# The first FFN product of a hybrid encoder block in Strassen's form, with the norm's factor applied at the end

## The chip, the core and the metric

The kernel runs on one core of one Trainium2 chip. The metric is device time in microseconds (us), as the median of several executions. TensorE (PE; PEld is its weight load) multiplies; VectorE (DVE), ScalarE (ACT) and GpSimd (POOL) do the elementwise work; SyncE (SP) issues the loads from HBM. Each engine takes its instructions in program order, and waits on semaphores for the others.

## The reference, cut to what matters

The input has 512 tokens of 1,024 features. 16 meta tokens are put ahead of them, so L is 528. The last third of the block is what changes:

```python
h = h + jnp.concatenate([y_ret, y_ssd], axis=-1) @ w_out[i]
u = _rmsnorm(h, norm2_w[i]) @ w_ff1[i]          # 1024 -> 4096
h = h + jnp.square(jax.nn.relu(u)) @ w_ff2[i]   # 4096 -> 1024
return _rmsnorm(h, final_norm_w)[:, CHUNK:]
```

Here `_rmsnorm(x, w)` is `x * rsqrt(mean(x*x) + 1e-6) * w` by token.

## The kernel before, in words

**Precision.** Every large product runs on operands split in two: hi is the value rounded to fp32r (an ACT copy, line 151), lo is what is left (a DVE subtraction, line 152). A block of 128 contraction rows then takes three matmuls: hi x hi, lo x hi and hi x lo. A weight load is 1 MB (`wr`, pool `wraw`, two buffers); each half of it is split into one tile `wh` of pool `whl` (three buffers).

**Stages, by the span's clock.** Up to about 420 us come the input projections, the SSD scan and the retention. The output projection `wo` follows in two halves of 512 columns (hf 0 to 470.6, hf 1 to 515.75), then the first FFN product to 697.58, then the second in two halves (`w2`) to about 877, and the last norm's tail.

**`token_gemm`** (wo and w2) holds four PSUM accumulators, one for each 128 tokens. For each of the 128-row blocks k it takes a split of the activations (`mh`, from `split_act`) as the stationary operand, and 512 columns of weights as the moving one. Its last `stag` blocks run as a tail, token block by token block, so that `fin` of one block runs beside the matmuls of the next. `weave` runs such a generator and, at each of its yields, one step of every job in `jobs`; `drain` runs the jobs to their end. So the program order on every engine is that of the emission.

**The first FFN product before.** `fin1` of a token block adds the accumulator to `xt` (line 802) and appends the job `norm_gen`, which applies the whole norm, waits `LAG` yields, transposes and splits into `hnh`/`hnl` (features on partitions). `first_tiles` computes three feature tiles of 128 by 256 tokens at a time (144 matmuls of 256 columns), because the last tokens come late; the other 29 tiles take 24 matmuls of 512 columns each (lines 334 to 336). `relu2` is an ACT relu out of PSUM and a DVE square into `a[f]`. `part`/`ahead` split one tile ahead of its use.

**Layout.** Pools with `side="right"` grow down from address 229,344, the others grow up from behind a scratch area of 16,384 bytes and 128 bytes of constants. From the tile sizes follow the start addresses in each partition: `whl` at 57,600, 66,304 and 75,008, and `mh2` (wo's hf 1) at 120,576 plus multiples of 4,096: all are multiples of 64. `mh` (wo's hf 0) at 154,144, `hnh` at 195,552, `hnl` at 212,448, `mhf` (w2) at 170,976, and of the retention `qr` at 174,752 and `kr` at 180,896 lie 32 bytes past a multiple of 64.

## Time and profile before

| | |
|---|---|
| median of 3 executions | 886.72 us (886.70 to 886.85) |
| profiled execution | 886.82 us, of which 885.0 us are the span from the first instruction to the last |
| mean granted TensorE clock | 0.997 of full speed |

The profile is of one execution. "Idle before" is the time for which an engine stood still ahead of an instruction, with what released it. A matmul's duration is longer than the distance to the next one's start, because matmuls overlap; so what a matmul costs is read from starts. PEclk 1.00 is 2.4 GHz, 0.50 is 1.2 GHz.

### The profile page before, as it was taken

The numbers are of one execution on the slowest core, as the hardware profiler recorded it, in microseconds if no ns is written. First come the engines' busy times: TensorE is split into PE (matmuls) and PEld (weight loads), VectorE is DVE, ScalarE is ACT, GpSimd is POOL, SyncE is SP. The second block draws the span as 40 slices with busy tenths as digits, with TensorE's granted clock in tenths as the row PEclk, the third lists the DMA queues.
The fourth block names the chain that finished last, engine by engine and source line by source line (L and its number), as shares of the span: only waits on it lengthen the run. The fifth ranks groups of instructions, "written<-read, shape, count | busy, mean of one in ns | idle before, by whom it ended". The sixth has DMA issues, their size and how long they took to land.

```text
span 885.0 us, 12244 instructions
## 1 busy us (share of the span) xinstructions
PE 873.3 (99%) x5062; PEld 757.9 (86%) x5062; DVE 488.9 (55%) x813; ACT 354.4 (40%) x602; POOL 34.0 (4%) x66
## 2 busy tenths in 40 slices
PE   8999999999999999999999999999999999999996
PEld 6999999989988999889888898888888888888884
DVE  5789887878654555445465563333333444464442
ACT  5673727372433232323454443222222333353332
POOL 2000000000000000000000010000000000000001
PEclk9999999999999999999999999999999999999998
DMA  8433241333231313222123431222222222222212
GB/s 324 147 122 96 96 127 65 100 93 108 60 96 48 96 51 93 62 81 96 49 96 96 143 119 33 93 90 90 93 89 94 96 94 90 95 94 95 95 49 95
DMA packets 84360, 85.14 MB, mean 96 GB/s; under 512 B 2352, under 2 KB 67120, under 8 KB 84304
## 3 DMA queue, kind: packets, MB, share of 16 engines
...
## 4 chain that ended last, share of the span: by engine, by line
PE 91%; DVE 3%; DMA 2%; ACT 2%; POOL 1%; issue 1%; POOLq 0%; SPq 0%; ACTq 0%; DVEq 0%
PE acc L765 9%; PE acc L763 9%; PE acc L764 9%; PE pf L335 7%; PE pf L336 7%; PE pf L334 7%; PE pz L457 3%; PE pj L334 3%; PE pj L336 3%; PE pj L335 3%; PE pv L334 2%; PE pk L336 2%; PE pv L336 2%; PE pk L334 2%; PE pk L335 2%; PE pv L335 2%
## 5 line engine op out<-in xcount | busy, mean ns | idle before, releaser
L152 DVE TENSOR_TENSOR wh<-wr,wh 128x1024 fp32r<-128x1024 f32 x134 | 163.5, 1221 | 137.4 <-ACT wh L151 137.4
L151 ACT ACTIVATE wh<-wr 128x1024 fp32r<-128x1024 f32 x134 | 141.0, 1055 | 204.0 <-PE acc L765 84.7
L763 PE MATMUL acc<-wh,mh 128*128 128x512 f32 x370 | 146.5, 396 | 0.0
L765 PE MATMUL acc<-wh,mh 128*128 128x512 f32 x370 | 146.0, 395 | 0.0
L764 PE MATMUL acc<-wh,mh 128*128 128x512 f32 x370 | 146.0, 395 | 0.0
L335 PE MATMUL pf<-hnl,wh 128*128 128x512 f32 (+1 forms) x280 | 105.4, 376 | 0.4 <-DVE hnl L152 0.4
L336 PE MATMUL pf<-hnh,wh 128*128 128x512 f32 (+1 forms) x280 | 105.6, 377 | 0.0
L334 PE MATMUL pf<-hnh,wh 128*128 128x512 f32 (+1 forms) x280 | 105.3, 376 | 0.0
L765 PEld LDWEIGHTS acc<-wh,mh 128*128 128x128 f32 x370 | 69.5, 188 | 16.5
L764 PEld LDWEIGHTS acc<-wh,mh 128*128 128x128 f32 x370 | 69.5, 188 | 16.2
L763 PEld LDWEIGHTS acc<-wh,mh 128*128 128x128 f32 x370 | 69.5, 188 | 16.1
L890 DVE TENSOR_TENSOR a<-r 128x512 f32<-128x512 f32 x32 | 22.2, 693 | 106.4 <-ACT r L889 106.4
L334 PE MATMUL pj<-hnh,wh 128*128 128x256 f32 (+2 forms) x256 | 73.6, 288 | 0.0
L336 PE MATMUL pj<-hnh,wh 128*128 128x256 f32 (+2 forms) x256 | 72.8, 286 | 0.0
L335 PE MATMUL pj<-hnl,wh 128*128 128x256 f32 (+2 forms) x256 | 72.8, 284 | 0.0
L889 ACT ACTIVATE r<-pf 128x512 f32<-128x512 f32 x32 | 19.1, 598 | 124.9 <-PE pf L336 124.9
L335 PEld LDWEIGHTS pf<-hnl,wh 128*128 128x128 f32 x280 | 53.0, 189 | 11.4 <-DVE hnl L152 0.7
L334 PEld LDWEIGHTS pf<-hnh,wh 128*128 128x128 f32 x280 | 52.7, 188 | 10.5
L336 PEld LDWEIGHTS pf<-hnh,wh 128*128 128x128 f32 x280 | 52.7, 188 | 10.1
L151 ACT ACTIVATE mh<-a 128x512 fp32r<-128x512 f32 x64 | 39.6, 623 | 34.3 <-PE acc L765 32.9
L152 DVE TENSOR_TENSOR mh<-a,mh 128x512 fp32r<-128x512 f32 x64 | 43.8, 689 | 14.7 <-ACT mh L151 14.7
L335 PEld LDWEIGHTS pj<-hnl,wh 128*128 128x128 f32 x256 | 48.2, 188 | 0.0
...
## 6 DMA issues: line engine op xcount, KB each, us to landing
wr<-in_w_ff_dram SPq DMA_DIRECT2D x32, 1024.0 KB, 5.1
...
wr<-in_w_out_dram SPq DMA_DIRECT2D x8, 1024.0 KB, 4.9
wr<-in_w_in_dram SPq DMA_DIRECT2D x7, 1024.0 KB, 4.9
...
```

Of the source, the lines that this page charges most:

```text
L151: ACT.activation(dst_h, src, AF.Copy)
L152: DVE.tensor_tensor(dst_l, src, dst_h.bitcast(F32), op=ALU.subtract)
L334: PE.matmul(ps[:, :n], lhsT=wh[:, k, :], rhs=hnh[:, k, t0:t0 + n], start=(k == 0), stop=False)
L335: PE.matmul(ps[:, :n], lhsT=wh[:, k, :], rhs=hnl[:, k, t0:t0 + n], start=False, stop=False)
L336: PE.matmul(ps[:, :n], lhsT=wl[:, k, :], rhs=hnh[:, k, t0:t0 + n], start=False, stop=(k == KT - 1))
L457: PE.matmul(o, lhsT=a[:, k, tk], rhs=zp[k // 4][y][:, k % 4, :], start=(i == 0), stop=(i == len(seq) - 1))
L763: PE.matmul(acc[b], lhsT=s[:, 0, tk], rhs=wh[:, kk, :], start=(k == 0), stop=False)
L764: PE.matmul(acc[b], lhsT=s[:, 1, tk], rhs=wh[:, kk, :], start=False, stop=False)
L765: PE.matmul(acc[b], lhsT=s[:, 0, tk], rhs=wl[:, kk, :], start=False, stop=(k == nk - 1))
L889: ACT.activation(r, ps, AF.Relu)
L890: DVE.tensor_tensor(a[f], r, r, op=ALU.mult)
```

## The change

The 4,096 features are taken in 8 groups of 512. In a group, weights and transposed tokens are seen as 2 x 2 blocks: contraction halves, feature halves (256) and token halves (256). Seven products of such blocks replace eight (Winograd's variant of Strassen's form). A product is 24 matmuls of 256 columns: two feature tiles by four contraction blocks by three split terms.

- **Tokens.** `tok_gen` replaces `norm_gen`: it transposes `xt` itself, and ACT copies it out of PSUM with norm2's weight as the scale (four copies of 128x128 for each transposed bank). Four DVE subtractions make the token sums, seven splits (`split_hs`) the operands `HS`.
- **Weights.** Each group has two 1 MB units. Four DVE sums (`s_sum`, 128x1024) per group are made partly in place in the raw tile, and each of the seven blocks is split (`w1_prep`), `LOOK` = 3 products ahead. A raw tile is free when product 3 (its first unit) or products 4 and 7 (its second) are split; only then are `next_loads` issued.
- **Sums of products.** Products 1 and 2 share a bank, 6, 7 and 4 another, 5 and 3 a third. Product 1 is copied out by ACT before product 2 accumulates in the same bank; products 6, 7 (two adds), 4 and 3 are added up by DVE. relu and square are both on ACT, one `product` later (`flush`), in place.
- **Norm.** The factor 1/(mean square + 1e-6) is made by `mean_sq` among the products and applied in `add_h2`, as the scale of the second FFN product's accumulator.
- **Order.** `seq` lists the products; the last two (4 and 3 of group 7) stand between the first steps of the second FFN product.
- **Memory.** `wraw` has 4 buffers, `whl` 4, `nwb` leaves `perm`, `pc` grows by 8 columns, `small` by four tiles, and the scratch area is 1,024 bytes.

```diff
-LAG = 4
+LAG = 2
+LOOK = 3
...
-PC_N = 104
+PC_CW, PC_CB, PC_SN, PC_RN, PC_N1, PC_N2 = 0, 64, 80, 88, 96, 104
+PC_N = 112
...
-    wraw = ctx.enter_context(tc.tile_pool(name="wraw", bufs=2))
-    whl = ctx.enter_context(tc.tile_pool(name="whl", bufs=3))
+    wraw = ctx.enter_context(tc.tile_pool(name="wraw", bufs=4))
+    whl = ctx.enter_context(tc.tile_pool(name="whl", bufs=4))
...
-    nwb = perm.tile([P, D], F32, name="nwb")
...
-    mh2 = tc.alloc_tile_pool(name="mh2", bufs=7, reuse_waits="tile")
+    mh2 = tc.alloc_tile_pool(name="mh2", bufs=6, reuse_waits="tile")
...
+    hnp.release()
...
+    NG = FF // 512
+    ar = tc.alloc_tile_pool(name="ar", bufs=1, side="right", reuse_waits="tile")
+    hs12 = tc.alloc_tile_pool(name="hs12", bufs=1, side="right", reuse_waits="tile")
     wx = tc.alloc_tile_pool(name="wx", bufs=3, side="right", reuse_waits="tile")
-    U[("w1", 0)].pools = [wx, wx]
...
+    HS = {q: hs12.tile([P, 2, 4, 256], F32R, name=f"hs{q}") for q in (1, 2)}
+    a_hi = ar.tile([P, 8, T], F32, name="a_hi")
+    R = [[a_hi[:, 2 * (2 * j + h):2 * (2 * j + h) + 2, :].rearrange("p a b -> p (a b)") for h in range(2)] for j in range(2)]
+    rs2 = [small.tile([P, 1], F32, name=f"rs2{b}", bufs=1) for b in range(NB)]
+    FP = {}
+    def split_hs(q, pool, src):
+        t = HS.get(q)
+        if t is None:
+            t = HS[q] = pool.tile([P, 2, 4, 256], F32R, name=f"hs{q}")
+        split(t[:, 0].rearrange("p k n -> p (k n)"), t[:, 1].rearrange("p k n -> p (k n)"), src)
+    def tok_gen(b):
         for _ in range(LAG):
             yield
-        transpose_split(xns[b], P, b * P)
+        h = b // 2
+        for j in range(2):
+            ps = psum(pm, "tp")
+            for k in range(4):
+                PE.transpose(ps[:, k * P:(k + 1) * P], xt[b][:, (4 * j + k) * P:(4 * j + k + 1) * P], ident)
+            dst = R[j][h].rearrange("p (k n) -> p k n", n=256)[:, :, (b % 2) * P:(b % 2 + 1) * P]
+            for k in range(4):
+                ACT.activation(dst[:, k, :], ps[:, k * P:(k + 1) * P], AF.Copy, scale=pc[:, PC_N2 + 4 * j + k:PC_N2 + 4 * j + k + 1])
+            if b == 1:
+                split_hs(1 + j, None, R[j][0])
+            yield
+        if b < 3:
+            return
+        sub = lambda o, x, y: DVE.tensor_tensor(o, x, y, op=ALU.subtract)
+        t2 = FP["a"][:, 14:16, :].rearrange("p a b -> p (a b)")
+        sub(R[0][0], R[0][1], R[0][0])
+        sub(t2, R[1][1], R[0][0])
+        while "t" not in FP:
+            yield
+        split_hs(6, FP["t"], t2)
+        yield
+        split_hs(5, FP["t"], R[0][0])
+        sub(R[0][1], R[1][1], R[0][1])
+        yield
+        split_hs(7, FP["t"], R[0][1])
+        yield
+        sub(R[1][0], R[1][0], t2)
+        split_hs(4, FP["t"], R[1][0])
+        yield
+        split_hs(3, FP["t"], R[1][1])
...
         add_h(1)(b, acc)
-        jobs.append(norm_gen(b))
-    ws = []
+        jobs.append(tok_gen(b))
...
+    seq = [(1, 0), (1, 1), (2, 0), (2, 1), (1, 2), (2, 2), (6, 0), (5, 0), (7, 0), (6, 1), (4, 0), (5, 1), (3, 0), (7, 1),
+           (6, 2), (4, 1), (5, 2), (3, 1), (7, 2)]
+    for g in range(3, NG):
+        seq += [(1, g), (4, g - 1), (6, g), (3, g - 1), (5, g), (2, g), (7, g)]
+    seq += [(4, NG - 1), (3, NG - 1)]
+    at = {q: i for i, q in enumerate(seq)}
+    raws, wsp, s1s = {}, {}, {}
+    loads = [0, 2, 4, 1, 6, 7] + list(range(8, 2 * NG))
...
+    def w1_load(u, raw=None):
+        if raw is None:
...
+        nc.sync.dma_start(out=raw.rearrange("p (k c) -> p k c", c=256),
+                          in_=w1[:, 256 * u:256 * (u + 1)].rearrange("(k p) c -> p k c", p=P))
+        raws[u] = raw
+    def next_loads():
+        while st1["load"] < len(loads) and (st1["load"] < 4 or loads[st1["load"] - 4] in done):
+            w1_load(loads[st1["load"]])
...
+    def quarter(g, r, c):
+        return raws[2 * g + r][:, c * 1024:(c + 1) * 1024]
+    def s_sum(i, g):
+        if i == 1:
+            s1s[g] = FP["s"].tile([P, 1024], F32, tag="s", name="s1")
+            DVE.tensor_tensor(s1s[g], quarter(g, 1, 0), quarter(g, 1, 1), op=ALU.add)
+        elif i == 3:
+            DVE.tensor_tensor(quarter(g, 1, 0), quarter(g, 0, 0), quarter(g, 1, 0), op=ALU.subtract)
+        elif i == 2:
+            DVE.tensor_tensor(quarter(g, 0, 0), s1s[g], quarter(g, 0, 0), op=ALU.subtract)
+        else:
+            DVE.tensor_tensor(quarter(g, 0, 1), quarter(g, 0, 1), quarter(g, 0, 0), op=ALU.subtract)
...
+    sums = {}
+    for g in range(NG):
+        p = at[(6, g)]
+        for i, q in ((1, p - 6), (3, p - 5), (2, p - 4), (4, max(p + 1, at[(2, g)] - LOOK + 1, at[(3, g)] - LOOK))):
+            sums.setdefault(max(q, 0), []).append((i, g))
+    def w1_prep(n, pool=None):
+        if n >= len(seq) or n in wsp:
+            return
+        q, g = seq[n]
+        src = {1: lambda: quarter(g, 0, 0), 2: lambda: quarter(g, 0, 1), 3: lambda: quarter(g, 0, 1), 4: lambda: quarter(g, 1, 1),
+               5: lambda: s1s[g], 6: lambda: quarter(g, 0, 0), 7: lambda: quarter(g, 1, 0)}[q]()
+        t = (pool or whl).tile([P, 2, 1024], F32R, tag="w", name="wh")
+        split(t[:, 0, :], t[:, 1, :], src)
+        wsp[n] = t.rearrange("p y (k c) -> p y k c", c=256)
+        if q == 3:
+            done.add(2 * g)
+        if all(at[(i, g)] in wsp for i in (4, 7)):
+            done.add(2 * g + 1)
+        next_loads()
...
     def before_tail():
...
+        next_loads()
+        for n in range(LOOK):
+            w1_prep(n, wx)
...
+    def a_block(g, r, h):
+        t, o = (FP["a"], 4 * g) if g < 6 else (a_hi, 4 * (g - 6))
+        return t[:, o + 2 * r:o + 2 * r + 2, h * 256:(h + 1) * 256]
...
+    def relu2(v, src=None):
+        ACT.activation(v, v if src is None else src, AF.Relu)
+        ACT.activation(v, v, AF.Square)
+    def flush():
+        while later:
+            relu2(later.pop(0))
+    def product(n):
+        for e in sums.get(n, ()):
+            s_sum(*e)
+        w1_prep(n + LOOK)
+        flush()
+        q, g = seq[n]
+        bk = {1: "a", 2: "a", 6: "b", 7: "b", 4: "b", 5: "d", 3: "d"}[q]
+        if q in (1, 6, 5):
+            banks[(bk, g)] = psum(pm if bk == "d" else pp, "f" + bk)
+        ps = banks[(bk, g)]
+        w, h = wsp[n], HS[q]
+        for t in range(2):
+            o = ps[:, t * 256:(t + 1) * 256]
+            cs = slice(t * P, (t + 1) * P)
+            for k in range(4):
+                for i, (y, z) in enumerate(((0, 0), (0, 1), (1, 0))):
+                    PE.matmul(o, lhsT=w[:, y, k, cs], rhs=h[:, z, k, :], start=(q in (1, 6, 5) and t == 0 and k == 0 and i == 0),
+                              stop=(k == 3 and i == 2), skip_group_check=True)
+            yield
+        pv = ps.rearrange("p (t n) -> p t n", n=256)
+        if q == 1:
+            ACT.activation(a_block(g, 1, 0), pv, AF.Copy)
+        elif q == 2:
+            relu2(a_block(g, 0, 0), pv)
+        elif q == 6:
+            DVE.tensor_tensor(a_block(g, 0, 1), pv, a_block(g, 1, 0), op=ALU.add)
+        elif q == 7:
+            v = a_block(g, 1, 1)
+            DVE.tensor_tensor(v, pv, a_block(g, 1, 0), op=ALU.add)
+            DVE.tensor_tensor(v, banks[("d", g)].rearrange("p (t n) -> p t n", n=256), v, op=ALU.add)
+            later.append(v)
+        elif q != 5:
+            v = a_block(g, 1, 0) if q == 4 else a_block(g, 0, 1)
+            DVE.tensor_tensor(v, pv, v, op=ALU.add)
+            later.append(v)
...
+    mh2.release()
...
     ap = tc.alloc_tile_pool(name="ap", bufs=1, reuse_waits="tile")
...
+    FP["a"] = ap.tile([P, 24, T], F32, name="a_lo")
+    FP["s"] = tc.alloc_tile_pool(name="fs", bufs=2, reuse_waits="tile")
+    for u, o in ((3, 16), (5, 20)):
+        w1_load(u, FP["a"][:, o:o + 4, :].rearrange("p a b -> p (a b)"))
...
+    def mean_sq(b):
+        jk = FP["s"].tile([P, D], F32, tag="s", name="jk")
+        ACT.activation(jk, xt[b], AF.Square, accum_out=rs2[b])
+        POOL.tensor_scalar(rs2[b], rs2[b], 1.0 / D, EPS, op0=ALU.mult, op1=ALU.add)
+        DVE.reciprocal(rs2[b], rs2[b])
+    def first_products():
+        for n in range(len(seq) - 2):
+            if n == LOOK:
+                wx.release()
+                FP["t"] = tc.alloc_tile_pool(name="hst", bufs=1, side="right", reuse_waits="tile")
+            if n == at[(6, 0)]:
+                drain()
+            if n in range(24, 24 + 4 * NB, 4):
+                mean_sq((n - 24) // 4)
+            yield from product(n)
...
+    def add_h2(hf):
+        def f(b, acc):
+            v = xt[b][:, hf * 512:(hf + 1) * 512]
+            DVE.scalar_tensor_tensor(v, acc, rs2[b], v, op0=ALU.mult, op1=ALU.add)
+        return f
...
+    FP["s"].release()
+    mhs = [tc.alloc_tile_pool(name="mhw", bufs=3, reuse_waits="tile")]
+    pre = [split_act(a_tile(k), mhs[0]) for k in range(3)]
+    second = token_gemm("w2", 0, 32, a_tile, fin_a, 2, mhs, pre, banks=(pp, pp, pp, pm))
+    for n in (0, 1):
+        weave(itertools.islice(second, 2 - n))
+        weave(product(len(seq) - 2 + n))
+    flush()
+    FP["t"].release()
+    hs12.release()
+    fin = tc.alloc_tile_pool(name="fin", bufs=1, side="right", reuse_waits="tile")
+    nwb = fin.tile([P, D], F32, name="nwb")
+    nc.sync.dma_start(out=nwb, in_=nfw.partition_broadcast(P))
+    mhs.append(tc.alloc_tile_pool(name="mhf", bufs=6, side="right", reuse_waits="tile"))
+    ys = tc.alloc_tile_pool(name="ys", bufs=1, reuse_waits="tile")
+    yo += [ys.tile([P, D], F32, name=f"yo{b}") for b in range(NB)]
+    ep += [ys.tile([P, 1], F32, name=f"ep{b}") for b in range(NB)]
+    weave(second)
+    weave(token_gemm("w2", 1, 32, a_tile, fin_b, 4, mhs))
     ys.release()
-    mh.release()
-    hnp.release()
-    fw.release()
+    mhs[1].release()
+    mhs[0].release()
+    fin.release()
+    ar.release()
     ap.release()
@@ -936,6 +1085,7 @@
     pcols[:, PC_SN:PC_SN + 8] = np.asarray(ssd_norm_w)[0].reshape(8, P).T
     pcols[:, PC_RN:PC_RN + 8] = np.asarray(ret_norm_w)[0].reshape(8, P).T
     pcols[:, PC_N1:PC_N1 + 8] = np.asarray(norm1_w)[0].reshape(8, P).T
+    pcols[:, PC_N2:PC_N2 + 8] = np.asarray(norm2_w)[0].reshape(8, P).T
     xall = np.concatenate([np.asarray(meta_tokens), np.asarray(x)[0]]).T.reshape(KT, P, L).transpose(1, 0, 2)
     xtr = np.concatenate([xall[:, :, :272].reshape(P, -1), xall[:, :, 272:].reshape(P, -1)], axis=1)
@@ -943,12 +1093,12 @@
     wzd = np.concatenate([wf[:, C_Z:C_Z + 256], wf[:, C_DT:C_DT + SH]], axis=1).reshape(2, 4, P, 256 + SH).transpose(2, 0, 1, 3)
     rope, mask, cpack, gpow = _constants()
     arrs = {
-        "x": f(x)[0], "meta_tokens": f(meta_tokens), "xtr": xtr, "wzd": wzd, "norm2_w": f(norm2_w)[0],
+        "x": f(x)[0], "meta_tokens": f(meta_tokens), "xtr": xtr, "wzd": wzd,
         "final_norm_w": f(final_norm_w), "w_in": f(w_in)[0], "w_out": f(w_out)[0], "w_ff1": f(w_ff1)[0],
         "w_ff2": f(w_ff2)[0],
         "hrows": np.concatenate([f(d_skip)[0], f(dt_bias)[0], f(a_log)[0]]), "pcols": pcols, "crope": rope, "cmask": mask, "cpack": cpack, "cident": np.eye(P, dtype=np.float32),
     }
-    nc = bacc.Bacc("TRN2", target_bir_lowering=False, num_devices=1)
```

## Rows read from the trace of the kernel before

**Rows 1.** The page: busy time, share of the span and instructions; chain by engine.

```profile
PE 873.3 (99%) x5062; PEld 757.9 (86%) x5062; DVE 488.9 (55%) x813; ACT 354.4 (40%) x602; POOL 34.0 (4%) x66
...
PE 91%; DVE 3%; DMA 2%; ACT 2%; POOL 1%; issue 1%; POOLq 0%; SPq 0%; ACTq 0%; DVEq 0%
```

**Rows 2.** TensorE's waits: waiting line, releaser, us in total, times, longest.

```profile
PE pf L335 <- DVE hnl L152: 0.4, 1, 0.4
```

**Rows 3.** Windows, first FFN product: stretch, length, busy time by engine, clock, DMA share, GB/s.

```profile
600.00:660.00 60.00, 60.00 (x258) 48.46 (x258) 19.87 (x21) 16.87 (x22) 0.00 (x0) 1.00 0.28 88
```

**Rows 4.** Matmuls of 512 columns by line and stretch: ns min/median/max, first and last start.

```profile
L763 PE MATMUL acc<-wh,mh x20: 395/396/397, 455.0 to 468.3; 128*128 128x512 f32 x20
...
L763 PE MATMUL acc<-wh,mh x22: 389/390/390, 471.1 to 485.4; 128*128 128x512 f32 x22
...
L763 PE MATMUL acc<-wh,mh x22: 392/396/397, 720.0 to 734.7; 128*128 128x512 f32 x22
...
L334 PE MATMUL pf<-hnh,wh x22: 392/394/399, 559.7 to 574.4; 128*128 128x512 f32 x22
```

**Rows 5.** Matmuls of 256 columns, first three tiles, the same columns.

```profile
L334 PE MATMUL pf<-hnh,wh x19: 278/280/282, 527.4 to 533.8; 128*128 128x256 f32 x19
```

**Rows 6.** Timeline of TensorE, 30 to 40 us: start, us, line, operation; 24 starts per shape.

```profile
30.48 0.28 PE L334 MATMUL pj<-hnh,wh 128*128 128x260 f32 x1
...
33.34 0.28 PE L334 MATMUL pj<-hnh,wh 128*128 128x256 f32 x1
...
36.18 0.29 PE L334 MATMUL pj<-hnh,wh 128*128 128x272 f32 x1
...
39.19 0.28 PE L334 MATMUL pj<-hnh,wh 128*128 128x256 f32 x1
```

**Rows 7.** Timeline of TensorE, z projection: 21 starts apart.

```profile
175.96 0.28 PE L457 MATMUL pz<-wh,hnl 128*128 128x256 f32 x1
...
178.45 0.28 PE L457 MATMUL pz<-wh,hnl 128*128 128x256 f32 x1
```

**Rows 8.** Matmuls of 128 columns of one retention head.

```profile
L705 PE MATMUL sc<-qr,kr x8: 274/275/276, 430.9 to 431.7; 128*128 128x128 f32 x8
```

**Rows 9.** VectorE by line and form: busy us, mean ns, idle before.

```profile
L152 DVE TENSOR_TENSOR wh<-wr,wh 128x1024 fp32r<-128x1024 f32 x134 | 163.5, 1221 | 137.4 <-ACT wh L151 137.4
L152 DVE TENSOR_TENSOR mh<-a,mh 128x512 fp32r<-128x512 f32 x64 | 43.8, 689 | 14.7 <-ACT mh L151 14.7
...
L802 DVE TENSOR_TENSOR xt<-xt,acc 128x512 f32<-128x512 f32 x16 | 10.7, 682 | 7.2 <-PE acc L765 7.2
```

**Rows 10.** Timeline of VectorE: two splits back to back, 1024 and 512 elements.

```profile
515.71 1.28 DVE L152 TENSOR_TENSOR hnl<-tp,hnh 128x512 fp32r<-128x512 f32 x2
...
517.50 2.35 DVE L152 TENSOR_TENSOR wh<-wr,wh 128x1024 fp32r<-128x1024 f32 x2
```

**Rows 11.** ScalarE by line and form, columns as for VectorE.

```profile
L151 ACT ACTIVATE wh<-wr 128x1024 fp32r<-128x1024 f32 x134 | 141.0, 1055 | 204.0 <-PE acc L765 84.7 <-PE pk L336 35.3 <-issue 31.9
...
L290 ACT ACTIVATE jk<-xt 128x1024 f32<-128x1024 f32 x4 | 4.2, 1056 | 0.1
```

**Rows 12.** The page and the DMA view: weight loads, KB, us from issue to landing.

```profile
wr<-in_w_ff_dram SPq DMA_DIRECT2D x32, 1024.0 KB, 5.1
...
GB/s 0 0 0 0 0 0 176 193 131 135 225 360 389 381 381 385 385 389 377 385 369 373 365 348 332 356 360 373 389 373 209 98 90 29 25 8 0 0 0 0
...
wr<-in_w_ff_dram SPq DMA_DIRECT2D x2, 1024.0 KB, 5.8
```

**Rows 13.** Windows at the end of the run, and the timeline's first row.

```profile
876.00:878.00 2.00, 0.95 (x5) 0.42 (x3) 0.59 (x1) 0.97 (x3) 0.81 (x2) 1.00 0.65 250
878.00:880.00 2.00, 0.00 (x0) 0.00 (x0) 0.76 (x2) 0.85 (x3) 0.30 (x2) 0.82 0.51 200
880.00:882.00 2.00, 0.00 (x0) 0.00 (x0) 0.75 (x1) 0.72 (x1) 0.51 (x1) 0.50 0.17 63
...
1.17 6.59 PE L135 MATMUL warm<-wz 128*128 128x512 bf16 x20 [1.17 <-DVE wz L129]
```

More of the change, by code (lines that the diff above doesn't have):

```diff
@@ L814 @@
     rw.release()
-    mh = mh2
-    xnp = tc.alloc_tile_pool(name="xnp", bufs=1, side="right", reuse_waits="tile")
-    wx = tc.alloc_tile_pool(name="wx", bufs=3, side="right", reuse_waits="tile")
-    U[("w1", 0)].pools = [wx, wx]
-    U[("w1", 1)].pools = [wx, whl]
-    H0, H1 = slice(0, 512), slice(512, 1024)
-    def first_half(b, o, e):
-        ss = small.tile([P, 1], F32, tag="ss", name="ss")
-        ACT.activation(o[:, H0], xt[b][:, H0], AF.Square, accum_out=ss)
-        POOL.tensor_scalar(e, ss, 1.0 / D, EPS, op0=ALU.mult, op1=ALU.add)
-        DVE.tensor_tensor(o[:, H0], xt[b][:, H0], nwb[:, H0], op=ALU.mult)
@@ new lines @@
+    loads = [0, 2, 4, 1, 6, 7] + list(range(8, 2 * NG))
+    st1 = {"load": 0, "ring": 0}
+    done = set()
+    def w1_load(u, raw=None):
+        if raw is None:
+            raw = wraw.tile([P, 2048], F32, tag="w", name="wr")
+        nc.sync.dma_start(out=raw.rearrange("p (k c) -> p k c", c=256),
[4 more added lines that the diff above has]
+            w1_load(loads[st1["load"]])
+            st1["load"] += 1
@@ L881 @@
     ap = tc.alloc_tile_pool(name="ap", bufs=1, reuse_waits="tile")
-    a = [ap.tile([P, T], F32, name=f"a{f}") for f in range(FF // P)]
-    fw = tc.alloc_tile_pool(name="fw", bufs=2, reuse_waits="tile")
-    mh = tc.alloc_tile_pool(name="mhf", bufs=6, side="right", reuse_waits="tile")
-    nc.sync.dma_start(out=nwb, in_=nfw.partition_broadcast(P))
-    def relu2(f, ps):
-        r = fw.tile([P, T], F32, tag="r", name="r")
-        ACT.activation(r, ps, AF.Relu)
-        DVE.tensor_tensor(a[f], r, r, op=ALU.mult)
@@ new lines, in fin_a @@
+    def fin_a(b, acc):
+        add_h2(0)(b, acc)
+        ss = small.tile([P, 1], F32, tag="ss", name="ss")
+        ACT.activation(yo[b][:, H0], xt[b][:, H0], AF.Square, accum_out=ss)
+        POOL.tensor_scalar(ep[b], ss, 1.0 / D, EPS, op0=ALU.mult, op1=ALU.add)
+        DVE.tensor_tensor(yo[b][:, H0], xt[b][:, H0], nwb[:, H0], op=ALU.mult)
+    def fin_b(b, acc):
+        add_h2(1)(b, acc)
+        ss = small.tile([P, 1], F32, tag="ss", name="ss")
+        rs = small.tile([P, 1], F32, tag="rs", name="rs")
+        ACT.activation(yo[b][:, H1], xt[b][:, H1], AF.Square, accum_out=ss)
+        POOL.tensor_scalar(rs, ss, 1.0 / D, ep[b], op0=ALU.mult, op1=ALU.add)
+        POOL.tensor_tensor(rs, rs, powc[:, 0:1], op=ALU.pow)
```

82 lines of the change are left out of this document (15 added, 67 removed).

## The prediction

> **What bounds the kernel now.** Read the page first: TensorE is busy for 873.3 us, 99% of the span, and 91% of the chain that ended last [rows 1]. Then its waits: at the start of the first FFN product it stood still once, for 0.4 us [rows 2], and nowhere behind that. So the stage lasts as long as its matmuls take to issue, and the other engines are half idle: in 60 us of it DVE worked 19.87 and ACT 16.87 us, at the full clock [rows 3]. The reader is to see two things: fewer matmul columns pay in full, and everything that the change puts on DVE is free only as long as its queue keeps ahead of TensorE.
>
> Next, what one matmul costs, from starts. 512 columns take 233.3 ns in wo's hf 0 (13.3 us over 19 x 3), in w2 and in the first FFN product (14.7 us over 21 x 3), but 227.0 ns (14.3 over 63) in wo's hf 1 [rows 4]. 256 columns take 118.5 ns in the first three tiles [rows 5] (the longer stretch of the next group gives 118.3, which I use).
>
> **Why 227 and 233.** By the addresses, wo's hf 1 is the one stage in which both operands start at multiples of 64 bytes; in the other three one of them is 32 bytes off. 6.3 to 6.7 ns is the time of 16 fp32 columns at 2.4 GHz, which are 64 bytes: an operand 32 bytes off touches one such line more. Shapes agree: 260 columns, offset so that they touch as many lines as 256 (17), take 119.2 ns (2.86/24) for 118.3 (2.84/24), while 272, with 18 lines, take 125.4 (3.01/24) [rows 6]. The z projection has its moving operand in place and its stationary one 32 off, and takes 118.6 ns (2.49/21) [rows 7], as if a line more cost the same on either side. At 128 columns both are off and nothing shows: 0.8 us for 7 gaps [rows 8].
>
> After the change the left stack starts from 1,024 + 128; `perm` loses 4,096 bytes and gains 32 in `pc`, 20,128 in all; `small` takes 640 and `wraw` 32,768. So `whl` starts at 54,688, 32 past a multiple of 64, and its tiles are multiples of 64: every weight tile is off. `hnh`, `mh`, `mhf` and the new `HS` tiles on the right stack are 32 off too. No stage of before runs large matmuls with both off. Bounds: nothing more (118.3 ns for 256), or a second line (118.3 + 6.7 = 125.0; 233.3 + 6.7 = 240.0). I take the second line, because either operand alone showed it.
>
> **The change part by part, TensorE.** Before, the first FFN product is 29 x 24 = 696 matmuls of 512 and 144 of 256 columns: 696 x 0.2333 + 144 x 0.1183 = 179.4 us. After, 8 x 7 x 24 = 1,344 of 256: 168.0 us at 125.0 ns (-11.4), or 159.0 at 118.3 (-20.4). The other stages move with the weight tiles: ahead of it 1,344 matmuls with one operand off get a second line (+9.0 us at 6.7 ns) and wo's hf 1 with 192 gets two (+2.5), in w2 768 get one (+5.1): +16.6, and +1.3 (192 x 6.7 ns) if only the first line counts. The 32 transposes stay as they were. Placement and columns together: +5.2, or -19.1.
>
> **DVE's work.** A group costs 11 operations of 1,024 elements (4 sums, 7 splits) and 5 adds out of PSUM. A lone split takes 1.221 us, the adds 0.682 [rows 9]; back to back two splits take 2.35 less what overlaps, some 1.14 each, and two halves 1.28, some 0.61 [rows 10]. 11 x 1.14 + 5 x 0.61 to 0.68 = 15.6 to 15.9 us, where TensorE needs 168 x 0.1183 = 19.9 or 168 x 0.125 = 21.0. That is four fifths of DVE, in a strict order with ACT (hi 1.055 us [rows 11]) and the loads. Three places are late.
>
> *Product (2, group 2).* It accumulates where (1,2) stands, so it waits for ACT's copy of (1,2). In ACT's queue that copy stands behind the hi of HS6, HS5, HS7 and HS4; HS7 waits for the subtraction R01, HS4 for R10, and these stand in DVE's queue behind sums and splits: from the last token block's add to R10 17 operations (5 weight sums, 4 token subtractions, 8 splits), 17 x 1.14 = 19.4 us and some 2.4 us of gaps for ACT and TensorE. The add comes about 21 us behind the start of wo's tail, R10 ends at 43, hi HS4 and the copy at 45. TensorE, with five products of 2.84 or 3.0 us, is there at about 36.5. Wait 8.4; bounds 0 (DVE catches up) and 9. I take 7.
>
> *The loop of the raw tiles.* From group 3 on: split of product 3 (hi, lo) frees both units; two loads of 1 MB; sum 1; then lo 7, add 3, sum 3, lo 1, sum 2, lo 4, lo 6 (8.6 us); the two adds of 7, sum 4, hi, lo (5.0). One load lands 5.1 us after its issue, two issued 2.2 us apart 5.8 each, at up to 389 GB/s [rows 12]; 2 MB issued together I put at 8.4 (between 5.1 + 2.5 = 7.6, a megabyte at that rate later, and 5.1 + 3.6). The circle is 22.0 us, TensorE's group 19.9 or 21.0: 1.0 or 2.1 us in each of four turns, 4 or 8.4 in all, below that nothing. I take 3.5 (8 where the pace is 118.3).
>
> *The second product's start.* Before, w2's first matmul follows without a wait. Now DVE makes two adds, three splits of activations (0.61 to 0.689 each [rows 9, 10]) and the weights' lo before the first step: about 4.1 us. At its fourth step the split stands on ACT behind relu and square of product 3, which wait for its add: about 3.2. Bounds 0 and 7.3, I take 6.
>
> Small ones: `mean_sq` puts a reciprocal in DVE's queue behind an ACT square (1.056 us [rows 11]) and a POOL operation, four times: 0 to 2, I take 1. The last tail has the same operations; the wait of 0.4 goes. `nwb`'s load moves behind the products on SP's queue, with 100 us until it is read: nothing.
>
> *The clock.* After the last matmul the granted clock goes from 1.00 to 0.82 and to 0.50, which is 1.2 GHz [rows 13]; how it would go in a wait of 7 us no row shows. The opening's 20 matmuls of 512 bf16 columns took 6.59 us [rows 13], against 20 x 0.2133 = 4.27 at 2.4 GHz: 2.3 us for one fall. Bounds 0 and 2.3, I take 1. The Trainium skill's page "TensorE: Matmul & The Clock Gate", section "HAM oscillation", says that gaps in which TensorE waits between bursts bring the low clock back, each time at a cost; the trace's end agrees (0.50), and this speaks against a change that puts waits into a stage without any.
>
> **Sum.** 5.2 + 7 + 3.5 + 6 + 1 + 1 - 0.4 = +23.3 us, on the profiled execution's 886.8 (0.1 above the median, of which 885.0 are span): **910 us**. Its own range goes from half the waits (901) to the whole walk (+5.2 + 9 + 4.4 + 7.3 + 2 + 2.3: 917).
>
> **Rivals.**
>
> *Placement costs no more when one operand is off already.* For it: 128 columns [rows 8], and that no row shows both. Against it: each operand alone costs a line. Then TensorE saves 19.1 and the loop is further behind: -19.1 + 7.5 + 8 + 6 + 1 + 1 - 0.4 = +4.0, 891 us; with waits a quarter smaller it ends below 885.0. The skill's page "TensorE: Matmul & The Clock Gate", section "Back-to-back issue gap", has a gap of N/2.4 + 2.5 ns, in which columns alone count: by that formula, which it gives for a lone matmul, an estimate of the first product goes from 165.9 to 146.7, -19.2, with no term for a start address. The trace has 227.0 and 233.3 for the same 512 columns, so part of the cost is not in that rule.
>
> *Only the difference of the two operands' places counts* (the other side). Both 32 off would then be as good as both in place: 512 columns at 227, and 256 at 111.7 (118.3 - 6.7, about the gap of 128 columns [rows 8]). The first product takes 1,344 x 0.1117 = 150.1 (-29.3), the matmuls ahead of it gain 1,344 x 6.7 ns = 9.0 and w2 5.1; the waits grow to some 30, as DVE and the loads set the pace: -29.3 - 14.1 + 30 - 0.4 = -13.8, 873 us. It decides as soon as wo's hf 0 shows 227 ns. For it: nothing but that the rows leave it open.
>
> *The waits are hidden, and placement costs nothing.* DVE has 4 us to spare per group, and the walk leans on 1.14 us; at 1.0 us per operation the circle falls to 20.7 and the copy of (1,2) comes 2.4 us sooner. -20.4 + 1.3 + at most 4: 868 to 872, I put 869. Against it: the copy's place behind HS4 stays.
>
> **Chances.** The forecast 0.50, the first rival 0.27 (a third of it ends faster), the second 0.11, the third 0.12. Faster by over 0.2% (below 885.0; less than that a measurement of this kernel hardly tells from no change): 0.09 + 0.11 + 0.12 = 0.32. Within 0.2%: 0.03, from the first rival. Slower: 0.65. The range leaves out the third rival and the upper end of the forecast, where all waits are at their bounds: 873 to 917.
>
> **What would show it.** In the profile after, a pace of 125 ns in the products and in the first projections and 240 in w2 (118.3 and 233.3: the first rival; 112 and 227: the second). A TensorE wait at the sixth product for ACT's copy, waits for DVE every 20 us or so, and two at w2's start; a granted clock below 1.00 behind the longest. DVE near 80% busy over the products. The forecast is wrong first through placement, 24 us between its ends, then through the waits, 0 to 25.

## The result: 866.0 us for 886.8, where 910 was forecast

| | before | changed |
|---|---|---|
| median | 886.79 us | 866.02 us (865.90 to 866.14, 4 executions) |
| ratio | | 0.9765 (95% interval 0.9748 to 0.9782) |
| span of the profiled execution | 885.0 us | 864.3 us, granted clock 0.998 |

The change made the kernel 20.8 us faster. The forecast of 910 us, its range (873 to 917) and its direction are wrong; of the rivals, the third (waits hidden, placement without cost, 869) was the nearest.

The page of the changed kernel, first the busy times [rows 1], then the two waits of TensorE that stand where the prediction had its large ones, from the view of waits:

```profile
PE 851.9 (99%) x5566; PEld 767.4 (89%) x5566; DVE 557.8 (65%) x872; ACT 406.6 (47%) x683; POOL 30.9 (4%) x58
```

```profile
PE acc L753 <- DVE mh L152: 0.4, 1, 0.4
...
PE fa L970 <- ACT a_lo L975: 0.3, 1, 0.3
```

TensorE is still busy all the time. The copy of (1,2) cost it 0.3 us (forecast 7), the start of w2 0.4 (forecast 6), the loop nothing (forecast 3.5). Next, in three views, the window over 50 us of products [rows 3], TensorE's timeline over one group, and w2 by its line [rows 4]:

```profile
600.00:650.00 50.00, 50.00 (x427) 50.00 (x426) 41.65 (x44) 32.44 (x42) 0.67 (x2) 1.00 0.29 87
```

```profile
613.45 5.82 PE L970 MATMUL fb<-hs,wh 128*128 128x256 f32 x48
619.10 5.82 PE L970 MATMUL fd<-hs,wh 128*128 128x256 f32 x48
```

```profile
L752 PE MATMUL acc<-wh,mh x22: 393/394/395, 720.3 to 735.0; 128*128 128x512 f32 x22
```

48 matmuls of 256 columns take 619.10 - 613.45 = 5.65 us, 117.7 ns each, though both operands lie 32 bytes past a multiple of 64; w2 stays at 233.3 ns (14.7 us over 63). DVE works 83% of the time, 16.5 us per group of 19.8, nearly the 15.6 to 15.9 forecast. So by its matmuls the first FFN product went from 179.4 to 1,344 x 0.1177 = 158.2 us, -21.2, and that is nearly the whole result: it begins at 515.64 us for 515.75, and from there to the end of the span there are 348.7 us for 369.3.

Two questions follow: why do the waits not appear, and what does an address cost?

### The profile page after: what moved, and what is told of

It is laid out like the page before. It is cut to its first block, busy times and chain, and to the rows that moved or that the text cites. A ratio compares the mean times of both kernels' runs of the same rounds, so it can differ in the third digit from the quotient of the medians.

```text
span 864.3 us, 13343 instructions
## 1 busy us (share of the span) xinstructions
PE 851.9 (99%) x5566; PEld 767.4 (89%) x5566; DVE 557.8 (65%) x872; ACT 406.6 (47%) x683; POOL 30.9 (4%) x58
## 4 chain that ended last, share of the span: by engine, by line
PE 91%; DVE 5%; ACT 1%; issue 1%; DMA 1%; POOL 1%; POOLq 0%; SPq 0%; DVEq 0%; ACTq 0%
PE acc L753 10%; PE acc L754 10%; PE acc L752 10%; PE fb L970 8%; PE fd L970 5%; PE pj L324 3%; PE pj L326 3%; PE pj L325 3%; PE fa L970 3%; PE pz L447 3%; PE pk L324 2%; PE pk L326 2%; PE pv L324 2%; PE pv L326 2%; PE pv L325 2%; PE pk L325 2%
## 5 line engine op out<-in xcount | busy, mean ns | idle before, releaser
L152 DVE TENSOR_TENSOR wh<-wr,wh 128x1024 fp32r<-128x1024 f32 x146 | 178.1, 1222 | 116.9 <-ACT wh L151 116.8
L970 PE MATMUL fb<-hs,wh 128*128 128x256 f32 x576 | 70.7, 280 | 0.1
L970 PEld LDWEIGHTS fb<-hs,wh 128*128 128x128 f32 x576 | 69.1, 188 | 0.3 <-DVE wh L152 0.3
L324 PEld LDWEIGHTS pj<-hnh,wh 128*128 128x128 f32 x256 | 48.3, 189 | 0.0
L326 PEld LDWEIGHTS pj<-hnh,wh 128*128 128x128 f32 x256 | 48.2, 188 | 0.0
L970 PE MATMUL fa<-hs,wh 128*128 128x256 f32 x384 | 47.8, 281 | 0.3 <-ACT a_lo L975 0.3
L970 PE MATMUL fd<-hs,wh 128*128 128x256 f32 x384 | 46.7, 280 | 0.0
L970 PEld LDWEIGHTS fa<-hs,wh 128*128 128x128 f32 x384 | 46.1, 189 | 0.4 <-ACT a_lo L975 0.4
L970 PEld LDWEIGHTS fd<-hs,wh 128*128 128x128 f32 x384 | 45.9, 188 | 0.1
L151 ACT ACTIVATE mh<-a_lo 128x512 fp32r<-128x512 f32 x48 | 29.4, 623 | 20.6 <-PE acc L754 18.3
L152 DVE TENSOR_TENSOR mh<-a_lo,mh 128x512 fp32r<-128x512 f32 x48 | 32.5, 687 | 8.9 <-ACT mh L151 8.9
```

The lines of the kernel that those rows point to most:

```text
L151: ACT.activation(dst_h, src, AF.Copy)
L152: DVE.tensor_tensor(dst_l, src, dst_h.bitcast(F32), op=ALU.subtract)
L324: PE.matmul(ps[:, :n], lhsT=wh[:, k, :], rhs=hnh[:, k, t0:t0 + n], start=(k == 0), stop=False)
L326: PE.matmul(ps[:, :n], lhsT=wl[:, k, :], rhs=hnh[:, k, t0:t0 + n], start=False, stop=(k == KT - 1))
L970: PE.matmul(o, lhsT=w[:, y, k, cs], rhs=h[:, z, k, :], start=(q in (1, 6, 5) and t == 0 and k == 0 and i == 0), stop=(k == 3 and i == 2), ...
```

## The experiments

All times are medians beside runs of the kernel before on the same chip (886.95 to 887.06 us).

### The waits: is the walk wrong, or the order that it walked?

ScalarE's timeline in the changed kernel, at the place of the first wait, shows that the order is another one:

```profile
531.22 0.59 ACT L975 ACTIVATE a_lo<-fa 128x512 f32<-128x512 f32 x1
...
532.64 1.06 ACT L151 ACTIVATE hs<-a_hi 128x1024 fp32r<-128x1024 f32 x1
534.38 1.06 ACT L151 ACTIVATE hs<-a_hi 128x1024 fp32r<-128x1024 f32 x1 [0.68 <-DVE a_hi L848]
```

The copy (line 975) runs ahead of the last splits of HS shown here; the code emits it behind those of HS7 and HS4. The framework that builds the program orders each engine's instructions anew. The sentence ahead of the prediction, that the program order on every engine is that of the emission, is false.

**e1: the order of emission.** 883.01 us, ratio 0.9955 (0.9940 to 0.9970).

```diff
+    by_hand = tc.manual_schedule()
+    by_hand.__enter__()
     weave(token_gemm("wo", 1, 16, mix_k, fin1, 6, [mh2], pre, before_tail))
...
         weave(product(len(seq) - 2 + n))
     flush()
+    by_hand.__exit__(None, None, None)
```

> The changed kernel with every engine's queue kept in the order in which the code emits it, from wo's second half to the start of w2; in the changed kernel itself ScalarE's copy of product (1,2) stands ahead of the splits of HS7 and HS4. Theory (my walk of the queues was right, only the order that it assumed is not the one that is built): TensorE waits about 8 us at product (2,2) for the copy, 1 to 2 us in each of four later groups, up to 7 us at the start of w2, so 10 to 25 us over the changed kernel, 876 to 891 us. Rival (the walk's durations or its dependencies are wrong, the order does not matter): within 2 us of the changed kernel, 866 to 868 us, and no wait over 1 us.

Its waits of TensorE at w2's start, its timelines of ScalarE and then of TensorE at the first wait, and its windows there and at w2's start (PEclk is the third number from the right):

```profile
PE acc L754 <- DVE wh L152: 1.8, 1, 1.8
...
PE acc L752 <- ACT wh L151: 1.0, 1, 1.0
```

```profile
533.64 1.06 ACT L151 ACTIVATE hs<-a_hi 128x1024 fp32r<-128x1024 f32 x1 [1.76 <-DVE a_hi L848]
538.19 1.06 ACT L151 ACTIVATE hs<-a_hi 128x1024 fp32r<-128x1024 f32 x1 [3.48 <-DVE a_hi L848]
539.15 0.58 ACT L975 ACTIVATE a_lo<-fa 128x512 f32<-128x512 f32 x1
```

```profile
539.78 4.98 PE L970 MATMUL fa<-hs,wh 128*128 128x256 f32 x24 [8.83 <-ACT a_lo L975]
544.60 1.57 PE L970 MATMUL fb<-hs,wh 128*128 128x256 f32 x12
```

```profile
532.00:536.00 4.00, 0.00 (x0) 0.00 (x0) 4.00 (x5) 1.06 (x1) 0.00 (x0) 0.72 0.00 0
536.00:540.00 4.00, 0.22 (x1) 0.22 (x2) 2.88 (x3) 1.81 (x3) 0.00 (x0) 0.50 0.00 0
540.00:544.00 4.00, 4.00 (x20) 4.00 (x20) 3.91 (x4) 1.62 (x2) 0.00 (x0) 0.50 0.00 0
544.00:546.00 2.00, 2.00 (x18) 2.00 (x18) 0.00 (x0) 1.17 (x3) 0.00 (x0) 1.00 0.00 0
...
684.00:686.00 2.00, 1.11 (x3) 0.92 (x4) 1.97 (x2) 0.00 (x0) 0.00 (x0) 0.50 0.16 60
```

In this order the first wait is there, at its place and of its size: 8.83 us for the 8.4 that the walk gave, and the copy stands behind both splits. The granted clock falls to 0.50, which is 1.2 GHz, in it, and the 24 matmuls from 539.78 to 544.60 take 4.82 us, 2.0 more than at 117.7 ns. By TensorE's starts e1 is then 10.3 us behind the changed kernel, and still so at its last products before w2 (668.97 for 658.67). At w2's start there are waits again (1.8, 1.0 and smaller ones) and a second fall of the clock, which together cost 7.0 us more, for the 6 of the forecast. The loop does not appear. 17.0 us in all: queues in emission order would have left 4 of the 21 us.

**e5: one instruction held back.** 866.19 us, ratio 0.9752 (0.9727 to 0.9778).

```diff
-            ACT.activation(a_block(g, 1, 0), pv, AF.Copy)
+            copy = ACT.activation(a_block(g, 1, 0), pv, AF.Copy)
+            if g == 2:
+                tc.add_manual_dep(copy.ins, FP["hi4"].ins.name, mybir.DependencyInfo(mybir.DependencyClass.NoSync, mybir.DependencyReason.SCHED_ONLY), reason="order")
```

(`FP["hi4"]` is the hi split of HS4.)

> The changed kernel with one instruction moved: ScalarE's copy of product (1,2) is held behind the hi split of HS4, where my walk had it. Theory (the place of this copy is what my first wait hung on): in the changed kernel's trace that split ends at 535.4 us and TensorE is ready for product (2,2) at 531.3, so it waits 4 to 5 us, loses up to 2 more to the clock, and nothing else moves: 870 to 873 us. Rival (the wait comes from VectorE's work as a whole and the other queues rearrange around it): under 1 us, 866 to 867 us.

My expectation missed, and its rival came true. TensorE's timeline:

```profile
527.77 3.34 PE L971 MATMUL fa<-hs,wh 128*128 128x256 f32 x28
530.95 2.88 PE L971 MATMUL fb<-hs,wh 128*128 128x256 f32 x24
533.66 1.98 PE L971 MATMUL fd<-hs,wh 128*128 128x256 f32 x16
536.26 3.09 PE L971 MATMUL fa<-hs,wh 128*128 128x256 f32 x24 [0.62 <-ACT a_lo L976]
```

TensorE's own order changed: product (6,0) in bank fb and part of (5,0) in fd run ahead of (2,2), which now comes 4 us later and still waits only 0.62 us. This one place in one queue, with the other queues left free, does not make the 8.8 us of e1; with all queues held the wait is there. Which of the others would suffice was not tried.

**e11: the loop as I had it.** 894.02 us, ratio 1.0077 (1.0060 to 1.0094). In e1's trace the two loads of a group are issued apart (SyncE's two issues from 620.14 us on stretch over 7.93 us): the first takes the buffer that products 4 and 7 have freed, the second the one that product 3 frees. The prediction had tied both to product 3. This kernel is e1 with

```diff
+        if u >= 8:
+            tc.add_manual_dep(dma.ins, st1["lo3"].ins.name, mybir.DependencyInfo(mybir.DependencyClass.Sync, mybir.DependencyReason.DATA), reason="order")
```

in `w1_load` (`lo3` is the lo split of the last product 3).

> The kernel with the queues in the order of emission once more, and both weight loads of a group held until the split of product 3, as my loop of the raw tiles had them; without that the trace shows them 6 to 8 us apart, because the first takes the buffer that products 4 and 7 free. Theory (the loop was right but for this): a circle of 22.0 us for TensorE's 19.8, so 2 us more in each of four groups, 883 + 7 to 9 = 890 to 892 us, with a wait of 1 to 3 us in each of them. Rival (the circle is shorter elsewhere too): 883 us, no new wait.

SyncE's issues, and the idle time of TensorE in its timeline:

```profile
587.23 0.99 SPq L885 DMA_DIRECT2D wr<-in_w_ff_dram  x2
610.09 0.99 SPq L885 DMA_DIRECT2D wr<-in_w_ff_dram  x2
634.05 0.99 SPq L885 DMA_DIRECT2D wr<-in_w_ff_dram  x2
656.24 0.99 SPq L885 DMA_DIRECT2D wr<-in_w_ff_dram  x2
```

```profile
605.94 5.89 PE L974 MATMUL fb<-hs,wh 128*128 128x256 f32 x48 [1.73 <-DVE a_lo L986]
...
629.90 7.28 PE L974 MATMUL fb<-hs,wh 128*128 128x256 f32 x48 [2.25 <-DVE a_lo L986]
```

From issue to issue the circle takes 22.9, 24.0 and 22.2 us for the 22.0 of the walk (in the longest the clock fell as well: the 48 matmuls behind the wait of 2.25 us take 7.28 us for 5.89). It costs 11.0 us over e1, 2 to 4 more than expected. With both assumptions put back, then, the waits are 894.0 - 866.0 = 28.0 us. The forecast's sum had 18.1, and with the loop at the pace that was measured (8 for 3.5) 22.6: the walk was not too pessimistic, it walked another program. In that program the change would have been 0.8% slower than the kernel before.

**e4: more work on VectorE.** 871.65 us, ratio 0.9827 (0.9810 to 0.9843).

```diff
+        if q in (1, 5, 7):
+            DVE.tensor_tensor(extra, xt[0], xt[1], op=ALU.subtract)
```

> The changed kernel with three more subtractions of 1,024 elements per group on VectorE, into a tile that nobody reads. Theory (VectorE has 3 to 4 us to spare in each group of 19.8 us, and the order of its queue is good enough to use them): 3 x 1.14 = 3.4 us more per group cost at most 3 us in all, 866 to 869 us. Rival (the queue has no slack where it counts, as my prediction's loop of the raw tiles had it): every microsecond more delays the loop, 8 x 3.4 = 27 us, 880 to 893 us.

Windows over the products:

```profile
535.00:550.00 15.00, 12.32 (x100) 11.70 (x99) 15.00 (x15) 5.24 (x6) 0.00 (x0) 1.00 0.23 71
550.00:600.00 50.00, 48.58 (x410) 48.06 (x410) 49.83 (x53) 31.42 (x43) 1.72 (x2) 1.00 0.24 77
600.00:650.00 50.00, 49.82 (x423) 49.62 (x422) 49.56 (x54) 34.20 (x46) 1.54 (x2) 1.00 0.36 114
```

In the steady groups (600 to 650) VectorE works 8 us more than in the changed kernel and TensorE is still busy 49.82 of 50: VectorE's spare time can be used nearly to the end. Counted in matmuls, TensorE does 27 fewer than in the changed kernel between 535 and 550 (100 for 127), 17 fewer in the next 50 us (410 for 427) and 4 fewer from 600 to 650: 48 x 0.1177 = 5.65 us, the whole loss. Most of it falls where the groups begin and VectorE has no spare time yet (15.00 of 15 already in the changed kernel); the longest waits there, 1.4 and 1.1 us, are for splits of weights. The 5.6 us are 2.6 more than the first theory allowed and a fifth of the rival's 27.

### The address: each operand's, or their distance?

**e2: the kernel before, both operands 32 bytes past a multiple of 64.** 881.95 us, ratio 0.9944 (0.9929 to 0.9959).

```diff
     powc = perm.tile([P, 4], F32, name="powc")
+    perm.tile([P, 4], F32, name="pad")
```

> The kernel before with 32 unused bytes ahead of its weight tiles, so that both operands of its large matmuls start 32 bytes past a multiple of 64. Theory of the prediction (an operand that is off costs 6.7 ns each time): 512 columns at 240 ns, 256 at 125 ns, +25 us, 912 us. Rival (no cost from a start address as such): 233.3, 227.0 in wo's second half and 118.3 as before, 886.7 us within 0.5. Second rival (the distance between the two operands decides, modulo some hundred bytes): 227.0 stays in wo's second half, where the distance stays a multiple of 512, and nothing else moves by more than 1 ns.

My line theory said +25 us; it became 5 us faster. The first rival's "as before" fails with it, and of the second only that the distance counts holds, not that nothing else moves. wo's first half and w2, from the views of one line:

```profile
L764 PE MATMUL acc<-wh,mh x19: 388/389/390, 455.3 to 467.5; 128*128 128x512 f32 x19
...
L764 PE MATMUL acc<-wh,mh x22: 387/389/389, 720.3 to 734.7; 128*128 128x512 f32 x22
```

12.2 us over 54 are 226 ns, 14.4 over 63 are 228.6, for 233.3 each [rows 4]. Nothing supports a price per operand.

**e8 and e10: TensorE alone.** Blocks of 48 and 72 matmuls, with the block's computation left out:

```python
w = 1024 * (i % 2) + m // 4      # moving operand, m bytes past a multiple of 512
c = P * (i % 6) + a // 4         # stationary operand, a bytes past one
PE.matmul(ps[:, :n], lhsT=high[:, c:c + P], rhs=low[:, w:w + n], start=(i == 0), stop=(i == 47))
```

> TensorE alone: 48 fp32r matmuls for each start address of the stationary operand (0 to 480 bytes past a multiple of 512) against a moving operand at 0, for each of six addresses shared by both, and for four of the moving one alone; first with 512, then with 256 columns. The block's computation is left out. Theory (the distance modulo 512 decides): 226.7 ns at distance 0 wherever both lie, up to 233.3 at 64 and 128, with values between at 32 and 256. Rival (in the kernel it is the other engines' reads): the same pace, within 1 ns, at every address.

The timeline names the blocks by columns (n) and moving address (m). In the first row of either width both operands have the same address, in the others the stationary one is at 0:

```profile
176.55 11.08 PE L102 MATMUL n512m32s<-low,high 128*128 128x512 f32 x48
...
242.02 11.36 PE L102 MATMUL n512m32s<-low,high 128*128 128x512 f32 x48
253.22 11.16 PE L102 MATMUL n512m64s<-low,high 128*128 128x512 f32 x48
264.22 11.32 PE L102 MATMUL n512m128s<-low,high 128*128 128x512 f32 x48
275.37 11.09 PE L102 MATMUL n512m256s<-low,high 128*128 128x512 f32 x48
...
365.86 5.92 PE L102 MATMUL n256m32s<-low,high 128*128 128x256 f32 x48
...
400.36 5.76 PE L102 MATMUL n256m32s<-low,high 128*128 128x256 f32 x48
405.96 5.61 PE L102 MATMUL n256m64s<-low,high 128*128 128x256 f32 x48
411.41 5.85 PE L102 MATMUL n256m128s<-low,high 128*128 128x256 f32 x48
417.10 5.90 PE L102 MATMUL n256m256s<-low,high 128*128 128x256 f32 x48
```

From here on, the distance is the start of the moving operand less that of the stationary one, modulo 256 bytes. (The expectations give it without its sign; all that were tried are multiples of 32.) At the same address, wherever that is, and at a distance of 256, 48 matmuls take the same time, and with 512 columns blocks of the same distance agree within 1 ns: there the distance decides. From the starts it gives 226.7 to 227.7 ns at 0, 229.0 at 64, 232.2 to 232.5 at 128, and 233.2 to 234.2 at 32, 96, 160, 192 and 224. So the sign counts: 64 bytes higher for the moving operand is 229 ns, 64 bytes higher for the stationary one (192) 233.4. The theory's modulus of 512 was wrong, and so were its values between at 32 and 256.

The rule of 256 columns is another. Distance 0 is the slowest (119.6 to 120.0 ns), and in two places the distance alone does not decide: at 64 one block took 113.4 and two, with the stationary operand at 192 and at 448, took 117.8; at 32 one took 116.7 and two 117.8.

> TensorE alone, 256 columns: 72 matmuls at each of eight start addresses, with the moving operand 64, then 32, then 160 bytes behind the stationary one's multiple of 256, then 64 again. The block's computation is left out. Theory (the distance decides, and at 64 there are two paces that a stream falls into): 64 gives 113.4 or 117.8 at either address, not the same in both passes; 32 and 160 give 116 to 120 at all of them. Rival (the absolute address decides which): at 64 the same addresses give 113.4 in both passes.

"Behind" means here at a higher address. At 64, with 256 columns, fifteen of the sixteen blocks took 117.8 ns, and the first of all, which begins with 21 steps of 213 ns, the same behind them; the 113.5 that e8 had (5.45 us over 48) at one of these addresses did not return at that address. 32 gave 116.7 to 116.8 in all eight blocks, 160 gave 117.3 but in its first (118.6). So the absolute address does not decide, and what puts a stream into the pace of 113.5 is open.

By this rule the kernel before reads otherwise. wo's second half had distance 0, its first half 224, w2 32, and the first product 32, 96, 160 and 224 in turn, as the 528 columns of a row of `hnh` are 2,112 bytes: 226.7, and 233 three times. e2 put wo's first half at 0 and w2 at 64. After the change w2 has 192 and still 233.3, HS has 64 and 117.7.

**e3, e6, e7, e9, e12: the distance set in the kernel.** Each is the changed kernel with unused bytes in a pool (e9's are the first and last line; e6 has 64 bytes under `a_hi` in place of e9's two, e7 those and the 128; e12 has 32 under `a_hi`, 32 in `fin` and the 128; e3 lays the six tiles `mh` of w2 at distances of their own):

```diff
+    rw.tile([P, 32], F32, name="gap", bufs=1)
...
     nwb = fin.tile([P, D], F32, name="nwb")
+    fin.tile([P, 16], F32, name="gap")
```

> The changed kernel with the six activation tiles of w2 laid at distances of 0, 32, 64, 128, 256 and 0 bytes, modulo 512, from the weight tiles (all six are 64 in the changed kernel). Theory (the distance decides): the matmuls on the two tiles at 0 go at 226.7 ns, those at 32 to 256 at 233.3, so w2 ends about 1.7 us sooner, 864.3 us. Rival (the region of the memory decides: the tiles that ran at 226.7 lay below 155,000, these lie above 183,000): all six at 233.3 ns, 866.0 us.

> The changed kernel with 64 unused bytes under a_hi, so that HS (first product) and the activation tiles of w2 lie at a multiple of 512 bytes from the weight tiles; they lay 64 bytes off it. Theory (the distance decides): w2's matmuls at 226.7 for 233.3 ns, 768 x 6.6 = 5.1 us, and the 1,344 of the first product at 112 to 114 for 117.7 ns, 5 to 8 us: 853 to 856 us. Rival (256 columns have a floor at 118, as the next-slower thing is the weight load): only w2 gains, 861 us. Third: a start address that is 32 off a multiple of 64 costs a line as predicted, nothing changes, 866 us.

> As the kernel before it in this list, and 128 unused bytes under the rope tables, so that wo's first half has its activation tiles at a multiple of 512 bytes from the weights too (128 off it in the changed kernel). Theory (the distance decides): 192 matmuls at 226.7 for 232.5 ns, 1.1 us less than the kernel before it. Rival: the same time.

> The changed kernel with 64 unused bytes under the last norm's weights and 128 under the rope tables: the activation tiles of w2 and of wo's first half lie at distance 0 (modulo 256) from the weight tiles, HS stays at 64. Theory (distance modulo 256 decides: at 0, 512 columns go at N + 32 cycles, 226.7 ns, but 256 columns at 120.0; 256 columns at distance 64 go at 117.7 or, in some executions, at 113.4): w2 gains 5, wo 1.1 us, the first product nothing: 860 us, and about 855 in executions with the faster pace. Rival: as with every stage at 0, 863 us.

> The kernel with distances set by stage, but HS at 32 in place of 64 (modulo 256) from the weight tiles, where TensorE alone took 116.7 ns in every case for 117.8 or 113.3. Theory: the first product takes 1,344 x 1.0 ns = 1.3 us less than in the slower of its two paces, 859.3 us, with all executions within 0.5 us of each other. Rival: two groups of executions about 5 us apart here too.

Distances in the table are of most matmuls of a stage; the first ones of HS and of w2, whose tiles come from other pools, lie at 0.

| | HS | w2 | wo's first half | median (executions) | ratio to before |
|---|---|---|---|---|---|
| changed kernel | 64 | 192 | 128 | 866.02 (865.9 to 866.1) | 0.9765 |
| e3 | 64 | 0, 224, 192, 128, 0, 0 | 128 | 861.62 (two at 859.2, two at 864.0) | 0.9714 (0.9685 to 0.9742) |
| e6 | 0 | 0 | 128 | 864.09 (864.05 to 864.12) | 0.9742 (0.9726 to 0.9758) |
| e7 | 0 | 0 | 0 | 863.16 (862.95 to 863.37) | 0.9732 (0.9717 to 0.9746) |
| e9 | 64 | 0 | 0 | 858.10 (855.53, 855.62, 860.58, 860.59) | 0.9665 (0.9636 to 0.9694) |
| e12 | 32 | 0 | 0 | 860.20 (859.49 to 861.07) | 0.9697 (0.9683 to 0.9712) |

TensorE's timeline over one group of products in e6, then in the profiled execution of e3, and w2 by its line in e9:

```profile
614.88 5.92 PE L971 MATMUL fb<-hs,wh 128*128 128x256 f32 x48
620.64 5.92 PE L971 MATMUL fd<-hs,wh 128*128 128x256 f32 x48
```

```profile
610.83 5.60 PE L970 MATMUL fb<-hs,wh 128*128 128x256 f32 x48
616.27 5.60 PE L970 MATMUL fd<-hs,wh 128*128 128x256 f32 x48
```

```profile
L754 PE MATMUL acc<-wh,mh x22: 389/389/389, 720.0 to 734.3; 128*128 128x512 f32 x22
```

e6: 5.76 us over 48, 120.0 ns; w2 gained its 5 us and the first product lost 1,344 x 2.3 ns = 3.1, together the 1.9 measured. My expectation of 112 to 114 at distance 0 was wrong, because I had only seen 0 with 512 columns. e7 is 0.9 us below e6, for 1.1 expected.

e3 answers its own question in its trace: its matmuls of w2 come in runs of twelve on one tile, which start 227.3, 227.7 and 226.7 ns apart on the tiles at distance 0, and 232.6, 233.2 and 233.2 on those at 224, 192 and 128 (the runs from 718.56 to 735.13 us). All six lie in the same region of the memory, so it is not the region. The slower of its two groups of executions, 864.0, is the expected 864.3.

The faster group, 4.8 us below, has another cause. The first product goes at 113.3 ns (5.44 over 48) in the trace of e3, with HS where the changed kernel has it. But the changed kernel's trace has both paces too. TensorE's timeline in the changed kernel, then in e3:

```profile
524.97 5.84 PE L970 MATMUL fa<-hs,wh 128*128 128x256 f32 x50
530.65 0.96 PE L970 MATMUL fb<-hs,wh 128*128 128x256 f32 x7
531.86 3.10 PE L970 MATMUL fa<-hs,wh 128*128 128x256 f32 x24 [0.25 <-ACT a_lo L975]
...
536.80 2.99 PE L970 MATMUL fd<-hs,wh 128*128 128x256 f32 x24
539.63 6.61 PE L970 MATMUL fb<-hs,wh 128*128 128x256 f32 x52
```

```profile
536.95 2.99 PE L970 MATMUL fd<-hs,wh 128*128 128x256 f32 x24
539.78 8.65 PE L970 MATMUL fb<-hs,wh 128*128 128x256 f32 x72
```

In the changed kernel 50 matmuls from 524.97 on take 113.6 ns each. Behind the wait of 0.25 us at 531.86 the pace is 117.9 (2.83 us over 24 from 536.80), and it stays so to the end. e3 does the same up to 539.78. There both have a pause (two starts 0.33 us apart), and behind it e3 goes on at 113.3 for some 1,100 matmuls. So a program and even an execution can have both paces, and at the one distance the pace changed only behind a break in the stream; what chooses it stays open. 1,100 x 4.5 ns = 4.9 us is what lies between the two groups, of e3 (4.8) and of e9 (5.0), and one of e5's four executions, 861.3 for 866.2, is as far off; as there is one trace of each kernel, the pace of the other executions is inferred from their times. e12 met neither of its expectations: its first products at distance 32 took 116.7 ns and those behind the breaks 117.7, and its executions are two pairs 1.4 us apart, about 1,100 x 1.0 ns.

In e9 w2 takes 14.3 us over 63, 227.0 ns, as in e6, with the first product at the changed kernel's distance. It is the fastest version, at the expected 860 and 855: 5.4 us under the changed kernel (860.6 for 866.0) by 192 bytes of padding, with the products at 117.7 ns in its trace, and 10.4 in the two executions that seem to have had the faster pace.

## Why the prediction was wrong

- **What bounds the kernel, and the columns: right.** TensorE's issue bounds it; 256 columns at 118.3 were measured at 117.7, and the term of -20.4 us for the columns at -21.2.
- **Placement: the step that failed first.** "I take the second line, because either operand alone showed it" put 24.3 us into the sum. The rows could not tell "an operand is off" from "the operands are at different distances": wo's second half was the only stage of large matmuls in which either theory has no cost. 260 and 272 columns fitted the line and proved nothing about it. e2 turned its sign, e8 gave the rule for 512 columns. The first rival was right that nothing is added here, but not in its reason, since e2 moved. The second was right that the distance counts, but took two operands 32 off a multiple of 64 as equally placed, where the period is 256: wo's first half, at 128, takes 232.5 ns. Its 111.7 ns at 256 columns was an extrapolation: distance 0 gives 120.0 there.
- **The three waits: the step "in ACT's queue that copy stands behind" failed, and with it the walk.** Durations and dependencies were good: with the emission's order 8.8 us were measured for 8.4, with both loads behind product 3 a circle of 22.2 to 24.0 for 22.0. But the order of a queue is not that of the emission, and which buffer a load takes is not what the walk assumed. The 18.1 us of waits and their clock cost in the sum were 0.7. Of the 44.1 us between forecast and result, 17.4 are this, and the rest placement and columns. (The upper end of the range takes 4.4 us for the loop where the walk gives 4; that changes nothing.)
- **w2's start** is of the same kind: 0.4 us, and in e1 7.0 with the fall of the clock, for 6.
- **VectorE's work: right,** 16.5 us per group for 15.6 to 15.9, at 1.14 us per operation. The third rival came nearest partly by luck: that placement adds nothing here and that the waits are hidden was right, but it hid them by operations of 1.0 us, and they were hidden by another order.
- **The clock:** no fall in the changed kernel, since there is no wait. In e1 it fell to 0.50 twice; the first cost 2.0 us on 24 matmuls, for a bound of 2.3. The Trainium skill's page "TensorE: Matmul & The Clock Gate", section "HAM oscillation", says that waits between bursts bring the low clock back, and on it I let the change count as risky. e1's trace agrees with it (0.50 in the wait of 8.8 us), and the changed kernel has no such wait. The formula in the same page's "Back-to-back issue gap" gave the first product -19.2 us as an estimate, 2 from the measured term. The 6.7 ns between the paces of the same 256 columns in e6 and e3 (120.0 and 113.3), 9.0 us over 1,344 matmuls, have no place in that formula.

What stays open: why a distance costs what it costs, and what decides between the two paces of 256 columns at 64 and at 32.
